# Encoder layer: norm weights spread by full-depth products, identity products ahead of them, first x tile in two halves

## The chip, the core and the metric

The kernel runs on one core of a Trainium2 chip. A core has five engines with a queue each, which run in order and wait for one another by semaphores: TensorE (PE; its weight loads are listed apart as PEld), VectorE (DVE), ScalarE (ACT), GpSimd (POOL) and SyncE (SP, which here issues all the DMAs). TensorE multiplies 128 rows deep, into PSUM, which has 8 banks of 128 x 512 float32. The metric is the time on the device in microseconds (us), the median of several runs.

## What is computed

The reference is one encoder layer, applied to two batches with shared weights: `x_prompt` (512 tokens) and `x_sample` (1024 tokens), 1024 channels, all float32. Cut to what matters here:

```python
def rmsnorm(x, g):
    y = x * lax.rsqrt(jnp.mean(x * x, axis=-1, keepdims=True) + EPS)
    return y * g

def encoder_layer(x, norm_g, w_in, ...):
    h = rmsnorm(x, norm_g)
    proj = h @ w_in                      # q, k, v, z of two attention branches, two gates
    ...                                  # neighbourhood attention (A), windowed attention (B)
    merged = sigmoid(ga) * oa + sigmoid(gb) * ob
    return x + merged @ w_out
```

The change touches how `h` of the prompt is begun: `norm_g` (1024 numbers, one for each channel) has to stand in every one of the 128 partitions, since a tile of x has 128 tokens in the partitions and the channels along the row.

## The kernel before, in words

The program has four phases: attention of the prompt, dense products of the prompt, then the same two for the sample. Float32 products are made of three products of `fp32r` parts: each operand is split into a high part (`whi`, `hh`; a copy on ACT) and a low part (`wlo`, `hl`; the operand less its high part, on DVE or POOL), and PE sums high by high, low by high and high by low (L764: three products for each of 8 depth steps, 24 for a tile of 128 tokens).

**The opening.** The prompt has four tiles `xt` of 128 tokens x 1024 channels (`norm_tile`, with t = 0 to 3). For a tile, in `rstd`: SP loads it (L460), ACT squares it with a running sum along the row (L463), POOL turns the sum into the mean plus epsilon (L467) and into the reciprocal root `nr` (L471). Then, in steps of 256 channels for t = 0 and of 512 for the others: DVE multiplies the tile by `nr` and by the norm weights (L523), PE transposes 128 x 128 pieces of it (L535, against the identity `ident`), ACT copies the transposed piece out of PSUM as `hh` (L540), and DVE makes `hl` (L545).

The norm weights get into all partitions in this way: SP loads them as one row of 1024 numbers into the first partition of the tile `rb` (L1799); PE multiplies a row of 128 ones (`one`, 1 x 128) by that row, in four products of 256 columns, one row deep (L1807), into two banks of PSUM; tile 0 reads the weights from PSUM (the `x` operand of its L523), and ACT copies each bank into `rb` (L1819), from where tiles 1 to 3 read them. A second copy of the weights, `gx`, holds the channels in the partitions (128 x 8, L1796). It is used in the sample's phase only, and its load has a late place in SP's queue.

The attention weights of the first group come in four pieces of 128 x 768 (L603; the first two into tiles `w`, the other two into tiles named `bias`), each split by ACT (`whi`, L605) and by DVE or POOL (`wlo`, L610). A tile's L764 needs pieces 1 to 4 in order, six products from each.

**What sets the order.** Nothing is issued as it is written. `Flow` collects all operations with a priority (the lower the sooner), their inputs and an estimated duration, then plays them through in its `run()`: at each planned moment an engine takes the ready operation with the lowest priority number, and where an operation has two engines to choose from (`wlo`, and other low parts and small sums), the one that is free sooner. So a new duration, or a new operation, moves others far behind it. The tables that matter here are `START` (priorities of the four loads of x), `NORM` (of the four tiles' work), `WAKE` and `WAKE_PRIO`. `wake()` puts `WAKE` groups of two PE instructions on the bank `d` ahead of other work; before, `WAKE` is 0, so that it puts none.

DMAs take 8 semaphores in turn, so SP holds the ninth DMA until the first has landed, and so on.

Of the kernel before, what the change touches and what calls it, by code (L numbers as in the profile page):

```python
# [29 lines left out]
SIDE = {5: 0, 8: 1, 11: 2, 15: 3}  # L30
CLASSIC_S = (0, 0, 0)
LEFT_PAD = 56
WAKE = 0
SOON = 10
RAW = {512: 2, 1024: 1}
WAKE_PRIO = 2
START = (-10, -6.5, -4, -3)
GATE = 2
FIRST_POOL = (0,)
# [1 line left out]
P = 128  # L41
# [313 lines left out]
def encoder_kernel(  # L355
# [4 lines left out]
    xt_p: bass.AP,  # L360
    xt_s: bass.AP,
    norm_g: bass.AP,
    norm_row: bass.AP,
    w_att: bass.AP,
    w_z: bass.AP,
    w_g: bass.AP,
# [49 lines left out]

    mhalf = cpool.tile([P, 8], F32, tag="mhalf", name="mhalf")
    dve.memset(mhalf, -0.5)
    one = cpool.tile([1, P], F32, tag="one", name="one")
    dve.memset(one, 1.0)  # L420
    gx = cpool.tile([P, KC], F32, tag="gx", name="gx")

    cpool.tile([P, LEFT_PAD], F32, tag="left_pad", name="left_pad")
# [18 lines left out]
    def wake():  # L442

        ps = bank("d")
        for i in range(WAKE):
            f.op(
                (("pe", 427),),
                lambda e, i=i: [pe.transpose(ps.t[:, j * P : (j + 1) * P], ident, ident) for j in range(2)],
                WAKE_PRIO, **({"into": [ps]} if i else {"new": [ps]}),
            )  # L450

    def rstd(pool, x, t, prio, load_prio, bufs, after=(), load_after=(), out=None):

        val = lambda shape, dt, tag, n: f.value(pool, shape, dt, tag, n)
        xt = val([P, D], F32, "xt", bufs)
        junk = val([P, D], mybir.dt.bfloat16, "junk", 1)
        ss, v = (val([P, 1], F32, "n" + n, bufs) for n in "sv")
        r = out or val([P, 1], F32, "nr", bufs)
        rv = lambda: r.t[:, t : t + 1] if out else r.t
        f.dma(lambda: nc.sync.dma_start(xt.t, x[t * P : (t + 1) * P, :]), 524288, load_prio, new=[xt], after=load_after)  # L460
        f.op(
            (("act", ACT_(D) + 93),),
            lambda e: act.activation(junk.t, xt.t, AF.Square, accum_out=ss.t), prio, new=[junk, ss], use=[xt], after=after,  # L463
        )
        f.op(
            (("pool", 164),),
            lambda e: nc.gpsimd.tensor_scalar(v.t, ss.t, 1.0 / D, EPS, op0=ALU.mult, op1=ALU.add),  # L467
            prio, new=[v], use=[ss],
        )
        f.op(  # L470
            (("pool", 464),), lambda e: nc.gpsimd.tensor_tensor(rv(), v.t, mhalf[:, :1], op=ALU.pow),  # L471
            prio, use=[v], **({"into": [r]} if out and t else {"new": [r]}),
        )
        return xt, r
# [1318 lines left out]


    f.stage(-1000, open=(r_h, d0["p"], rb_pool, early["p"], late["p"], norm_p), make=h_p)
    f.dma(lambda: nc.sync.dma_start(gx, norm_g), 4096, 1, into=[gx_v])  # L1796
    wake()
    gb = f.value(rb_pool, [P, NT_S], F32, "rb", 1)
    row = f.dma(lambda: nc.sync.dma_start(gb.t[:1], norm_row.unsqueeze(0)), 4096, START[0] + 0.1, new=[gb])  # L1799
    gains_row = []  # L1800
    for i in range(2):
        ps, made = bank("x"), []
        for j in range(2):
            cols, out = slice(i * 512 + j * 256, i * 512 + j * 256 + 256), slice(j * 256, j * 256 + 256)
            made.append(f.op(
                (("pe", 850),),
                lambda e, ps=ps, cols=cols, out=out: pe.matmul(ps.t[:, out], one, gb.t[:1, cols], start=True, stop=True),  # L1807
                NORM[0] - 1, hold=[gb], after=[row], **({"into": [ps]} if j else {"new": [ps]}),
            ))
        gains_row.append([ps, made])  # L1810
    for t in range(gp.nb):
# [64 lines left out]
def _layout(inp):  # L1876
# [15 lines left out]
    for m in range(8):  # L1892
# [11 lines left out]
        "xt_p": inp["x_prompt"][0][gp.perm].T.reshape(KC, P, NT_P),  # L1904
        "xt_s": inp["x_sample"][0][gs.perm].T.reshape(KC, P, NT_S),
        "norm_g": inp["norm_g"][0].reshape(KC, P).T,
        "norm_row": inp["norm_g"][0],
        "w_att": np.stack(groups),
        "w_z": np.stack(w_z),
        "w_g": np.stack(w_g),  # L1910
# [39 lines left out]
```

## Time and profile before

| | |
|---|---|
| runs, us | 1136.4, 1136.74, 1139.61 |
| median, us | 1136.74 |
| the profiled execution, us | 1139.25 |
| its span, first to last instruction, us | 1137.5 |
| mean granted TensorE clock | 0.998 of full |
| instructions | 18703 |
| bytes read and written in HBM | 137.66 MB and 51.92 MB |

A profile is one execution. Its pages list each engine's busy time; the view of waits says what ended an engine's idle time; the chain follows the work that ended last back from the last instruction; the timeline lists instructions by their start; the view by windows gives busy time of each engine in a stretch. Times are us from the first instruction. L numbers are lines of the kernel before; in the changed kernel the same lines stand from 1 line higher to 17 lines lower (L460 is L467, L463 is L474, L523 is L536, L535 is L548, L540 is L553, L545 is L558, L605 is L618, L610 is L623, L764 is L777, L1807 is L1825, L1819 is L1837).

### The profile page before, as it was taken

To read this page: it belongs to the slowest core of one execution; us is meant where nothing else is said; L and a number is where in the kernel's file an instruction comes from. 1 tells how busy PE (TensorE), PEld (TensorE's weight loads), DVE (VectorE), ACT (ScalarE), POOL (GpSimd) and SP (SyncE) were. 2 spreads that over 40 slices of the span, in tenths; PEclk is the share of its full clock that TensorE was granted. 3 is DMA by queue.
4 is the path that set the end of the run, shared out by engine and by line. 5 is a ranking of instruction groups with operands and counts; after the bars stand their busy time and mean duration, and the time that the engine had idled before them with its cause. 6 is when DMAs were issued, how large, how long until landed. Compare 5 with 4: busy or idle time off the path is not lost.

```text
span 1137.5 us, 18703 instructions
## 1 busy us (share of the span) xinstructions
PE 1121.8 (99%) x6079; PEld 975.1 (86%) x6079; DVE 856.8 (75%) x1988; ACT 651.4 (57%) x1499; POOL 339.3 (30%) x438
## 2 busy tenths in 40 slices
PE   8999999999999999999999999999999999999998
PEld 6999988888888889999999988988788888888877
DVE  5878797587776568787878889876988766767564
ACT  5777987644532247565769888877543435333430
POOL 3654433000011144434324343510333323123111
PEclk9999999999999999999999999999999999999999
DMA  7854543488785743121213214244888645756862
GB/s 257 273 159 138 185 115 103 107 254 257 246 286 202 249 138 91 29 61 29 82 41 93 73 38 119 50 131 138 288 261 237 206 158 191 278 197 224 262 208 93
DMA packets 139108, 186.11 MB, mean 164 GB/s; under 512 B 29897, under 2 KB 68561, under 8 KB 139010
## 3 DMA queue, kind: packets, MB, share of 16 engines
q1 hardware_dynamic: 139010, 184.91, 51.8%
q8 instruction: 48, 0.79, 0.3%
q14 instruction: 50, 0.41, 0.1%
HBM read 137.66 MB, written 51.92 MB: 167 GB/s over the span
## 4 chain that ended last, share of the span: by engine, by line
PE 90%; DMA 4%; DVE 2%; ACT 1%; issue 1%; SPq 1%; POOL 0%; ACTq 0%; DVEq 0%
PE p L764 26%; PE x L1293 8%; PE x L1295 8%; PE x L1294 8%; PE x L1066 5%; PE x L1029 5%; PE x L937 5%; PE p L1294 4%; PE p L1295 4%; PE p L1293 4%; PE d L1293 4%; PE d L1295 4%; PE d L1294 4%; PE x L864 2%; DMA w<-in_w_att_dram 1%; DMA U<-m_d 1%
## 5 line engine op out<-in xcount | busy, mean ns | idle before, releaser
L764 PE MATMUL p<-whi,hh 128*128 128x384 f32 x384 | 133.7, 348 | 0.0
L764 PE MATMUL p<-whi,hl 128*128 128x384 f32 x384 | 132.6, 345 | 0.0
L764 PE MATMUL p<-wlo,hh 128*128 128x384 f32 x384 | 132.0, 344 | 0.0
L1172 ACT ACTIVATE whi<-raw 128x512 fp32r<-128x512 f32 (+1 forms) x140 | 81.5, 600 | 73.0 <-PE x L1294 22.5
L981 ACT ACTIVATE sb<-sb,mx 128x384 f32<-128x384 f32 (+1 forms) x192 | 107.7, 565 | 16.9 <-DVE mx L972 16.6
L1294 PE MATMUL x<-T,whi 128*128 128x512 f32 x280 | 108.9, 389 | 0.0
L1293 PE MATMUL x<-T,whi 128*128 128x512 f32 x280 | 108.9, 389 | 0.0
L1295 PE MATMUL x<-T,wlo 128*128 128x512 f32 x280 | 108.9, 389 | 0.0
L764 PE MATMUL p<-whi,hb 128*128 128x384 f32 x384 | 107.6, 346 | 0.0
L1177 DVE TENSOR_TENSOR wlo<-raw,whi 128x512 fp32r<-128x512 f32 (+1 forms) x110 | 73.4, 678 | 34.5 <-ACT whi L1172 31.0
L1177 POOL TENSOR_TENSOR wlo<-raw,whi 128x512 fp32r<-128x512 f32 (+1 forms) x30 | 36.4, 1219 | 210.2 <-ACT whi L1172 210.2
L1040 DVE TENSOR_TENSOR pp<-x,pp 128x512 fp32r<-128x512 f32 (+1 forms) x136 | 82.6, 639 | 19.2 <-ACT pp L1035 18.5
L802 POOL TENSOR_TENSOR rs_r<-rs_v,mhalf 128x4 f32<-128x4 f32 (+1 forms) x72 | 80.7, 1121 | 5.7
L1293 PE MATMUL x<-hh,whi 128*128 128x512 f32 x200 | 78.4, 392 | 2.1 <-ACT fh L1440 2.1
L1035 ACT ACTIVATE pp<-x 128x512 fp32r<-128x512 f32 (+1 forms) x136 | 70.9, 561 | 15.2 <-PE x L1029 14.0
L1295 PE MATMUL x<-hh,wlo 128*128 128x512 f32 x200 | 78.5, 393 | 0.0
L1294 PE MATMUL x<-hl,whi 128*128 128x512 f32 x200 | 78.3, 392 | 0.0
L1066 PE MATMUL x<-pp,v 128*128 128x256 f32 (+1 forms) x368 | 75.8, 322 | 0.0
L764 PEld LDWEIGHTS p<-whi,hl 128*128 128x128 f32 x384 | 72.8, 190 | 1.3 <-issue 1.0
L764 PEld LDWEIGHTS p<-wlo,hh 128*128 128x128 f32 x384 | 73.0, 190 | 1.0 <-issue 0.7
L764 PEld LDWEIGHTS p<-whi,hh 128*128 128x128 f32 x384 | 73.0, 190 | 0.7 <-DVE v L812 0.3
L764 PEld LDWEIGHTS p<-whi,hb 128*128 128x128 f32 x384 | 69.1, 188 | 3.0 <-issue 1.3
(388 smaller groups left out, 2967.8 us busy)
## 6 DMA issues: line engine op xcount, KB each, us to landing
raw<-in_w_g_dram SPq DMA_DIRECT2D x84, 256.0 KB
w<-in_w_att_dram SPq DMA_DIRECT2D x46, 384.0 KB
raw<-in_w_z_dram SPq DMA_DIRECT2D x40, 256.0 KB
ot<-o_d SPq DMA_DIRECT2D x36, 256.0 KB
g_d<-C SPq DMA_DIRECT2D x34, 256.0 KB
fr<-in_w_g_dram SPq DMA_DIRECT2D x28, 256.0 KB
raw<-in_w_out_dram SPq DMA_DIRECT2D x28, 256.0 KB
out_dram<-C SPq DMA_DIRECT2D x19, 256.0 KB
```

The lines of the kernel that those rows point to most:

```text
L764: pe.matmul(ps.t[:, :GW], part[u](k), mv.t[:, c], start=k == 0 and m == 0, stop=k == KC - 1 and m == 2,)
L802: lambda e: nc.gpsimd.tensor_tensor(r.t[:, :nn], rv.t[:, :nn], mhalf[:, :nn], op=ALU.pow),
L937: pe.matmul(pss[2 * pair + i].t[:, :width], q.t[rows, u, at : at + P], kv[:, tiles[0] : tiles[-1] + 1 : step], start=n == 0, stop=n == 2,)
L981: act.activation(sb.t[:, :width], sb.t[:, :width], AF.Exp, bias=mx.t[:, i : i + 1], scale=-1.0, accum_out=sm.t[:, i : i + 1],)
L1035: lambda e, pt=pt, pp=pp, nn=nn: act.activation(pp.t[:, 0, :nn], pt.t[:, :nn], AF.Copy),
L1040: lambda e, pt=pt, pp=pp, nn=nn: dve.tensor_tensor(pp.t[:, 1, :nn], pt.t[:, :nn], pp.t[:, 0, :nn].bitcast(F32), op=ALU.subtract),
L1066: pe.matmul(out(), v.t[:, vs], mv(), start=first, stop=last)
L1172: (("act", ACT_(n)),), lambda e: act.activation(hi(), src(), AF.Copy), prio,
L1177: lambda e: engines[e].tensor_tensor(lo(), src(), hi().bitcast(F32), op=ALU.subtract), prio,
L1293: pe.matmul(out, hi.t[:, cs], mh(), start=first and k == 0, stop=False, **more)
L1294: pe.matmul(out, hi.t[:, cs], ml(), start=False, stop=False, **more)
L1295: pe.matmul(out, lo.t[:, cs], mh(), start=False, stop=last and k == len(ws) - 1, **more)
```

## The change

- `norm_row` is no longer an input. `gx` is loaded second instead, behind the first half of the first x tile.
- DVE multiplies the identity by each of the 8 columns of `gx`: eight diagonal tiles, side by side in `rb` (128 x 1024). The four products multiply a full 128 x 128 tile of ones by them: each result column is the sum of one diagonal column, which is the weight of that channel, in all partitions.
- `WAKE` is 6 and `WAKE_PRIO` -30: 12 products of the identity by itself, 128 x 128, float32, go first on PE. Before, the (unused) code had transposes there.
- The first tile of the prompt is loaded and squared in two halves of 512 columns, with two sums (`ns`, `nt`), which POOL adds in the instruction that adds epsilon. The factor 1/1024 moves from POOL into the scale of the Square (1/32) for all tiles, the sample's too.

```diff
-WAKE = 0
+WAKE = 6
...
-WAKE_PRIO = 2
+WAKE_PRIO = -30
...
-    one = cpool.tile([1, P], F32, tag="one", name="one")
-    dve.memset(one, 1.0)
+    ones = cpool.tile([P, P], F32, tag="ones", name="ones")
+    dve.memset(ones, 1.0)
...
-                lambda e, i=i: [pe.transpose(ps.t[:, j * P : (j + 1) * P], ident, ident) for j in range(2)],
+                lambda e, i=i: [
+                    pe.matmul(ps.t[:, j * P : j * P + P], ident, ident, start=True, stop=True) for j in range(2)
+                ],
...
+        halves = 1 if out or t else 2
+        loads, n = [], D // halves
+        for i in range(halves):
+            c = slice(i * n, i * n + n)
+            loads.append(f.dma(
+                lambda c=c: nc.sync.dma_start(xt.t[:, c], x[t * P : (t + 1) * P, c]), 512 * n, load_prio + 0.2 * i,
+                after=load_after, **({"hold": [xt]} if i else {"new": [xt]}),
+            ))
+        for i in range(halves):
+            c = slice(i * n, i * n + n)
+            f.op(
+                (("act", ACT_(n) + 93),),
+                lambda e, i=i, c=c: act.activation(junk.t[:, c], xt.t[:, c], AF.Square, scale=1.0 / 32, accum_out=sums[i].t),
...
-            lambda e: nc.gpsimd.tensor_scalar(v.t, ss.t, 1.0 / D, EPS, op0=ALU.mult, op1=ALU.add),
+            (lambda e: nc.gpsimd.tensor_scalar(v.t, ss.t, sums[1].t, EPS, op0=ALU.add, op1=ALU.add)) if halves == 2 else
+            (lambda e: nc.gpsimd.tensor_scalar(v.t, ss.t, 1.0, EPS, op0=ALU.mult, op1=ALU.add)),
...
-    f.dma(lambda: nc.sync.dma_start(gx, norm_g), 4096, 1, into=[gx_v])
+    f.dma(lambda: nc.sync.dma_start(gx, norm_g), 4096, START[0] + 0.1, into=[gx_v])
...
-    row = f.dma(lambda: nc.sync.dma_start(gb.t[:1], norm_row.unsqueeze(0)), 4096, START[0] + 0.1, new=[gb])
...
+            for k in (4 * i + 2 * j, 4 * i + 2 * j + 1):
+                diag = f.op(
+                    (("dve", 68 + 0.68 * P),),
+                    lambda e, k=k: dve.tensor_scalar(gb.t[:, k * P : k * P + P], ident, gx[:, k : k + 1], None, op0=ALU.mult),
...
-                lambda e, ps=ps, cols=cols, out=out: pe.matmul(ps.t[:, out], one, gb.t[:1, cols], start=True, stop=True),
+                lambda e, ps=ps, cols=cols, out=out: pe.matmul(ps.t[:, out], ones, gb.t[:, cols], start=True, stop=True),
```

The planner's estimate for a weight product goes from 850 to 450 ns. What the program now issues is shown at three places, all at the very start. On PE, before (a name is `out<-inputs`; `rb` the weights' row, `p` the projection):

```order
L1807 MATMUL x<-rb,one 128x256 x4
L535 MATMUL x<-ident,xt 128x128 x8
L764 MATMUL p<-whi,hh 128x384
L764 MATMUL p<-wlo,hh 128x384
L764 MATMUL p<-whi,hl 128x384
```

and in the changed program:

```order
L448 MATMUL d<-ident 128x128 x12
L1825 MATMUL x<-rb,ones 128x256 x4
L548 MATMUL x<-ident,xt 128x128 x6
L777 MATMUL p<-whi,hh 128x384
L777 MATMUL p<-wlo,hh 128x384
L548 MATMUL x<-ident,xt 128x128 x2
L777 MATMUL p<-whi,hl 128x384
```

The identity products stand first, and two products of the projection now stand ahead of the last two transposes of tile 0. Behind these rows, tile 1's eight transposes have moved from among tile 0's products to behind the last of them.

On ACT at the start, before (`junk,ns<-xt` is the Square; the one of 128x1024 in the sixth row is that of tile 1):

```order
L463 ACT_TABLE_LOAD
L463 ACTIVATE junk,ns<-xt 128x1024
L605 ACTIVATE whi<-w_124 128x768
L605 ACTIVATE whi<-w_126 128x768
L1819 ACTIVATE rb<-x 128x512
L463 ACTIVATE junk,ns<-xt 128x1024
L540 ACTIVATE hh<-x 128x2x128 x3
L605 ACTIVATE whi<-bias 128x768
L540 ACTIVATE hh<-x 128x2x128
L605 ACTIVATE whi<-bias 128x768
L1819 ACTIVATE rb<-x 128x512
```

and in the changed program:

```order
L474 ACT_TABLE_LOAD
L474 ACTIVATE junk,ns<-xt 128x512
L474 ACTIVATE junk,nt<-xt 128x512
L618 ACTIVATE whi<-w_133 128x768
L618 ACTIVATE whi<-w_137 128x768
L553 ACTIVATE hh<-x 128x2x128 x3
L1837 ACTIVATE rb<-x 128x512 x2
L618 ACTIVATE whi<-bias 128x768
L553 ACTIVATE hh<-x 128x2x128
L618 ACTIVATE whi<-bias 128x768
L474 ACTIVATE junk,ns<-xt 128x1024
```

The Square of tile 1 has moved from ahead of the first `hh` to behind the fourth `whi`, and both copies of the weights stand together behind the third `hh`.

On DVE at the start, before:

```order
L418 MEMSET mhalf 128x8
L420 MEMSET one 1x128
L523 SCALAR_TENSOR_TENSOR xt<-xt,nr,x 128x256 x2
L610 TENSOR_TENSOR wlo<-w_126,whi 128x768
L523 SCALAR_TENSOR_TENSOR xt<-xt,nr,x 128x256 x2
L545 TENSOR_TENSOR hl<-x,hh 128x2x128 x3
L523 SCALAR_TENSOR_TENSOR xt<-xt,nr,rb 128x512
L610 TENSOR_TENSOR wlo<-bias,whi 128x768
```

and in the changed program:

```order
L419 MEMSET ones 128x128
L1819 TENSOR_SCALAR rb<-ident,gx 128x128 x8
L536 SCALAR_TENSOR_TENSOR xt<-xt,nr,x 128x256 x4
L623 TENSOR_TENSOR wlo<-w_137,whi 128x768
L558 TENSOR_TENSOR hl<-x,hh 128x2x128 x3
L640 TENSOR_SCALAR gq<-gcol 128x2
L623 TENSOR_TENSOR wlo<-bias,whi 128x768
L558 TENSOR_TENSOR hl<-x,hh 128x2x128
L623 TENSOR_TENSOR wlo<-bias,whi 128x768
L536 SCALAR_TENSOR_TENSOR xt<-xt,nr,rb 128x512 x2
```

The second piece's `wlo` has moved behind all four multiplications of tile 0, and the two of tile 1 behind the `wlo` of the fourth piece.

On SP the loads of the weights' row and of the whole first tile are replaced by those of the first half, of `gx` and of the second half; then the order is the same for the next ten loads, without the later one of `gx`. Further back the order of DVE, ACT, POOL and SP differs through the prompt's attention and into its dense products, and some 19 operations move from DVE to POOL; from the later part of the prompt's dense products to the end it is the same on every engine.

More of the change, by code (lines that the diff above doesn't have):

```diff
@@ L362, in encoder_kernel @@
     norm_g: bass.AP,
-    norm_row: bass.AP,
     w_att: bass.AP,
@@ L456, in rstd @@
         junk = val([P, D], mybir.dt.bfloat16, "junk", 1)
-        ss, v = (val([P, 1], F32, "n" + n, bufs) for n in "sv")
+        ss, v, s2 = (val([P, 1], F32, "n" + n, 1 if n == "t" else bufs) for n in "svt")
+        sums = [ss, s2]
         r = out or val([P, 1], F32, "nr", bufs)
         rv = lambda: r.t[:, t : t + 1] if out else r.t
[L460 to L464, printed above, removed]
+        halves = 1 if out or t else 2
[11 more added lines that the diff above has]
+                lambda e, i=i, c=c: act.activation(junk.t[:, c], xt.t[:, c], AF.Square, scale=1.0 / 32, accum_out=sums[i].t),
+                prio, use=[xt], after=[*after, loads[i]], **({"new": [sums[1]], "into": [junk]} if i else {"new": [junk, ss]}),
+            )
         f.op(
             (("pool", 164),),
-            lambda e: nc.gpsimd.tensor_scalar(v.t, ss.t, 1.0 / D, EPS, op0=ALU.mult, op1=ALU.add),
-            prio, new=[v], use=[ss],
+            (lambda e: nc.gpsimd.tensor_scalar(v.t, ss.t, sums[1].t, EPS, op0=ALU.add, op1=ALU.add)) if halves == 2 else
+            (lambda e: nc.gpsimd.tensor_scalar(v.t, ss.t, 1.0, EPS, op0=ALU.mult, op1=ALU.add)),
+            prio, new=[v], use=sums[:halves],
         )
@@ L1795, in encoder_kernel @@
     f.stage(-1000, open=(r_h, d0["p"], rb_pool, early["p"], late["p"], norm_p), make=h_p)
-    f.dma(lambda: nc.sync.dma_start(gx, norm_g), 4096, 1, into=[gx_v])
+    f.dma(lambda: nc.sync.dma_start(gx, norm_g), 4096, START[0] + 0.1, into=[gx_v])
     wake()
     gb = f.value(rb_pool, [P, NT_S], F32, "rb", 1)
-    row = f.dma(lambda: nc.sync.dma_start(gb.t[:1], norm_row.unsqueeze(0)), 4096, START[0] + 0.1, new=[gb])
-    gains_row = []
+    gains_row, diag = [], None
     for i in range(2):
@@ L1803, in encoder_kernel @@
         for j in range(2):
+            for k in (4 * i + 2 * j, 4 * i + 2 * j + 1):
+                diag = f.op(
+                    (("dve", 68 + 0.68 * P),),
+                    lambda e, k=k: dve.tensor_scalar(gb.t[:, k * P : k * P + P], ident, gx[:, k : k + 1], None, op0=ALU.mult),
+                    NORM[0] - 1, use=[gx_v], **({"hold": [gb]} if k else {"new": [gb]}), after=[diag],
+                )
             cols, out = slice(i * 512 + j * 256, i * 512 + j * 256 + 256), slice(j * 256, j * 256 + 256)
             made.append(f.op(
-                (("pe", 850),),
-                lambda e, ps=ps, cols=cols, out=out: pe.matmul(ps.t[:, out], one, gb.t[:1, cols], start=True, stop=True),
-                NORM[0] - 1, hold=[gb], after=[row], **({"into": [ps]} if j else {"new": [ps]}),
+                (("pe", 450),),
+                lambda e, ps=ps, cols=cols, out=out: pe.matmul(ps.t[:, out], ones, gb.t[:, cols], start=True, stop=True),
+                NORM[0] - 1, hold=[gb], after=[diag], **({"into": [ps]} if j else {"new": [ps]}),
             ))
@@ L1906, in _layout @@
         "norm_g": inp["norm_g"][0].reshape(KC, P).T,
-        "norm_row": inp["norm_g"][0],
         "w_att": np.stack(groups),
```

## The prediction

> **What bounds the kernel now.** I read the page first, then the waits of the tensor engine (PE), then the chain that ended last, then the opening in order of time. The page's first part:
>
> ```profile
> PE 1121.8 (99%) x6079; PEld 975.1 (86%) x6079; DVE 856.8 (75%) x1988; ACT 651.4 (57%) x1499; POOL 339.3 (30%) x438
> ```
>
> PE is busy for 1121.8 of 1137.5 us, so a change can only win by removing PE idle time (15.7 us in all) or by making PE's own instructions shorter. The view of waits (who waited for what: us in total, times, longest) for PE:
>
> ```profile
> PE x L1807 <- DMA rb<-in_norm_row_dram: 4.6, 1, 4.6
> PE x L864 <- DVE qk L819: 2.4, 2, 1.9
> PE x L1293 <- ACT fh L1440: 2.1, 1, 2.1
> PE d L1294 <- DVE T L1177: 1.3, 1, 1.3
> PE x L535 <- DVE xt L523: 1.0, 1, 1.0
> PE p L1293 <- ACT whi L1172: 0.5, 1, 0.5
> ```
>
> The first and fifth row are the opening: 5.6 us. The others lie later; two rows of 0.2 follow. Then the chain over the opening (start, us, what):
>
> ```profile
> 1.94 6.16 DMA w<-in_w_att_dram
> ...
> 8.11 0.85 ACT whi L605
> ...
> 8.99 0.96 DVE wlo L610
> 9.95 0.40 DVE xt L523
> ...
> 10.39 1.15 PE x L535 x4
> 11.54 4.45 PE p L764 x15
> ```
>
> The second weight piece lands at 8.09; its low part (`wlo`, L610) stands on DVE ahead of the last two multiplications of x tile 0 (L523), and so holds PE's last four transposes until 10.39. From about 11.2 on PE has work without a break. But it is slow work at first. Rows of the timeline (start, duration):
>
> ```profile
> 14.86 0.52 PE L764 MATMUL p<-whi,hl 128*128 128x384 f32 x1
> ...
> 15.47 0.34 PE L764 MATMUL p<-wlo,hh 128*128 128x384 f32 x1
> ...
> 15.65 0.34 PE L764 MATMUL p<-whi,hl 128*128 128x384 f32 x1
> ...
> 18.65 0.35 PE L764 MATMUL p<-whi,hl 128*128 128x384 f32 x1
> ```
>
> Until 15.2 one product follows the other after 0.32 us (15 in 4.45 us, with the change near the end), from 15.47 on after 0.175 us. That is a clock at half rate, which the granted clock does not show here (it reads 1.00) but does show near the end of the kernel:
>
> ```profile
> 5.19:8.60 3.41, 3.41 (x10) 2.29 (x9) 0.87 (x2) 1.53 (x4) 2.53 (x3) 1.00 1.00 396
> 8.60:12.01 3.41, 2.40 (x11) 1.83 (x10) 2.84 (x7) 3.39 (x8) 0.75 (x2) 1.00 0.97 365
> 404.60:408.02 3.42, 2.12 (x10) 1.38 (x8) 2.81 (x5) 2.61 (x4) 3.25 (x3) 1.00 0.91 314
> 1083.79:1087.20 3.41, 1.32 (x6) 1.04 (x6) 1.93 (x4) 1.64 (x3) 0.00 (x0) 1.00 0.77 290
> 1087.00:1088.00 1.00, 1.00 (x4) 0.83 (x3) 0.77 (x2) 0.00 (x0) 0.00 (x0) 0.60 0.27 100
> 1090.00:1091.00 1.00, 1.00 (x5) 0.78 (x4) 0.87 (x2) 0.63 (x1) 0.00 (x0) 0.69 0.22 41
> ```
>
> (Stretch, length, then busy us of PE, PEld, DVE, ACT, POOL, then the granted clock.) 0.60 in 1087 to 1088 and 0.69 in 1090 to 1091 put the half rate from 1087.2 to 1090.6: one window of 3.4 us, after a window in which PE was busy for 1.32 of 3.41 us; and it ended after one full window. [...] In 5.19 to 8.60 PE was busy all the time with the products of one row (L1807), and still ran at half rate until 15.4. So such products did not raise the rate; the products of full depth (L764, from 11.2) did, 4.2 us later.
>
> [...]
>
> **The change, part by part.** These rows carry the durations (start, us, engine):
>
> ```profile
> 0.99 0.29 POOL masks.py:199 TENSOR_SCALAR_AFFINE_SELECT ident<-ident 128x128 f32<-128x128 f32 x1
> ...
> 4.29 1.06 ACT L463 ACTIVATE junk<-xt 128x1024 bf16<-128x1024 f32 x1 [2.30 <-DMA xt<-in_x_p_dram]
> ...
> 4.59 3.75 PE L1807 MATMUL x<-rb,one 1*128 1x256 f32 x8 [4.59 <-DMA rb<-in_norm_row_dram]
> ...
> 4.80 0.45 SPq L1796 DMA_DIRECT2D gx<-in_norm_g_dram  x1
> ...
> 5.25 0.19 ACT L463 ACTIVATION_READ_ACCUMULATOR junk<-xt 128x1 f32 x1
> ...
> 5.80 0.57 POOL L471 TENSOR_TENSOR nr<-nv,mhalf 128x1 f32<-128x1 f32 x1
> ...
> 6.86 0.87 DVE L523 SCALAR_TENSOR_TENSOR xt<-xt,nr,x 128x256 f32<-128x256 f32 x2 [5.86 <-PE x L1807]
> ...
> 8.86 0.58 ACT L1819 ACTIVATE rb<-x 128x512 f32<-128x512 f32 x1
> ...
> 10.51 0.99 ACT L540 ACTIVATE hh<-x 128x256 fp32r<-128x256 f32 x3
> ...
> 10.91 1.09 DVE L545 TENSOR_TENSOR hl<-x,hh 128x256 fp32r<-128x256 f32 x3 [0.18 <-ACT hh L540]
> ...
> 11.91 0.74 DVE L523 SCALAR_TENSOR_TENSOR xt<-xt,nr,rb 128x512 f32<-128x512 f32 x1
> ...
> 16.46 0.60 ACT L540 ACTIVATE hh<-x 128x512 fp32r<-128x512 f32 x1 [2.73 <-PE x L535]
> ...
> 17.09 0.69 DVE L545 TENSOR_TENSOR hl<-x,hh 128x512 fp32r<-128x512 f32 x1 [1.70 <-ACT hh L540]
> ```
>
> *The identity products.* They need only the identity, ready at 1.28, so PE starts near 1.45. Each float32 product is two passes: L1807's four are x8 in the trace. Eight passes of 256 columns take 3.75 us, about 0.446 each with the last one's drain left out; 128 columns are half, 0.223; 24 passes take 5.35 us and end at 6.8 at half rate. If they count as work, the rate rises 3.4 to 6.8 us after 1.45, at 5.0 to 8.3; I take the middle, 6.6, so they end at 6.7.
>
> *The weight products* now wait for them, not for a transfer: 6.7 against 4.59. At full rate eight passes of 0.223 end at 8.5. L523 began at 6.86, 0.49 us after the fourth pass of 0.446 from 4.59; now that is 6.7 + 0.89 + 0.45 = 8.05. The four multiplications of tile 0 then run in one piece, 0.475 each, to 9.95. Ahead of them lie eight multiplications of the identity on DVE. No row has that form; the nearest:
>
> ```profile
> L1013 DVE TENSOR_SCALAR sb<-sb,rs 128x256 f32<-128x256 f32 x33 | 11.0, 383 | 0.2
> ...
> L669 DVE TENSOR_SCALAR qk<-p,rs_r 128x128 f32<-128x128 f32 x5 | 1.7, 343 | 0.0
> ```
>
> Half of the first is 0.19 us, the second 0.34: eight take 1.5 to 2.7 us, and from the landing of `gx` (an estimate: near 4.0, behind the first half tile, since the whole tile had landed at 4.29) they end by 5.5 to 6.7. I take the lower, from SBUF like the new ones. The identity products hide either; without them the upper end would set the start of the last two weight products.
>
> *The x tile in two halves.* Half the data lands sooner (an estimate: 0.7 us, half of what 512 KB take), so the first Square runs under the second load. Two Squares of 0.60 (the 128x512 row) and two read-outs of 0.19 make 1.58 us against 1.25; the reciprocal root is ready near 6.1 against 6.37. With the weights at 8.05 this is worth nothing, and if the identity products were gone, at most 0.3 us. On SP one issue more, and `gx` (0.45) in the row's place (0.32), put the weight pieces back by some 0.5 us: the second lands at 8.6, its high part ends at 9.45, before DVE asks for it at 9.95.
>
> *What stands late now.* DVE: second `wlo` 9.95 to 10.9, then `hl` of tile 0, the first at 11.3; PE's third product needs it and starts at 11.6 (before: 11.98). From there 0.174 us each, with two short stalls for the `wlo` of the third and fourth piece: on ACT the third `hh` ends at 10.3, the two copies of the weights (L1819) at 11.5, third `whi` 12.35, fourth `hh` 12.7, fourth `whi` 13.55; on DVE the matching `wlo` end at 13.35 and 14.7. Tile 0's 24 products end at 15.8; before, with the eight transposes of tile 1 (0.9 us) already done, at 18.3. This is a lead of 1.6 us. But ACT now squares tile 1 only behind the fourth `whi`: 13.55 to 14.8 against 9.46. Then the root (0.93 us from the read-out, as 5.44 to 6.37), 15.75; two multiplications of 0.74, to 16.5 and 17.25; transposes, `hh` at 17.2 to 17.8; DVE has a sum and a copy (0.40 and 0.28) ahead of `hl`, 17.95 to 18.65. Tile 1's third product starts at 18.9; before, at 18.65. **The lead is gone**: PE idles 1.9 us of 15.8 to 18.9.
>
> Behind that the rows of PE are as dense as before, in another order; walked with the same durations, tile 2's products end 0.15 later. Before, the next thing was the shorter of the two waits for `qk` (2.4 less 1.9 is 0.5 us); now nine products of L1293 to L1295 stand ahead of those transposes and cover it. **Sum: +0.15 - 0.5, about -0.35 us.** The profiled execution took 1139.25 us (span 1137.5), so 1138.9. The runs shown lie at 1136.4, 1136.74 and 1139.61: two levels, and the profiled one is at the upper. I carry the difference to the median: 1136.4. The late landing at 8.09 may belong to the upper level alone; without it the old opening gains up to 0.9 (its second piece is then no longer on the path), the new one little, so the difference may be +0.5 at the median.
>
> **The rivals.**
>
> *The lead lasts.* If ACT's copies or the Square come sooner than I lay them out, the lead of 1.6 and the 0.5 stay: 1134.6; with the rate up at its earliest, 5.0, the identity products end 0.8 sooner: 1133.8. Against it: ACT's order is fixed and its rows sum as above.
>
> *The rate falls back.* Its place is the thin stretch from 15.8 to 18.9. The rows above bound the point where it decides: a window with 1.30 us idle of 3.42 (404.60) kept the rate, one with 2.09 idle lost it (1083.79). [...] The price: half rate until a window has filled again, 3.4 to 6.8 us, in the middle 16 products of 0.146 us more, 2.3 us: 1138.7, at most 3.1 us, 1139.5. This one is slower. [...]
>
> *It does not warm.* Float32 passes of an identity may count as little as the one-row products. Then the weight products end at 6.8 + 3.57 = 10.4, the last multiplication at 11.8, 1.85 later than above, and all behind it: 1138.2.
>
> *The new order costs.* Some 400 us of DVE, ACT, POOL and SP are in another order. In the waits above, the 0.5 of `qk` and the 0.5 of L1293 are all of any size that lies there; one more wait of the 1.9 or 2.1 us kind or two gives 1138.5 to 1140.5.
>
> **How the numbers follow.** Forecast 0.44, lead lasts 0.14, rate falls 0.16, no warming 0.12, order 0.14. 0.3% is 3.4 us, about what a measurement can tell from no change. Faster by more needs the whole lead and an early rate: 0.06. Slower by more: the upper ends of the fall and of the order, 0.09. Within: 0.85. The range reaches from the lead with an early rate, 1133.8, to the upper ends of the fall and the upper level of the runs, 1139.7.
>
> **What would show it.** Right: identity products from 1.4 to about 6.7; weight products over by 8.5; products 0.175 us apart from the first; Square of tile 1 at 13.5; PE idle near 16 to 18.9. Wrong: products 0.32 us apart after 12 (no warming) or after 18 (a fall); tile 1's third product before 18; new rows among PE's waits between 30 and 400 us.

## The result, and the profile after

| | before | after |
|---|---|---|
| median, us | 1136.74 (1136.4 to 1139.82) | 1148.6 (1145.06 to 1149.27) |
| after over before | | 1.0085, 95% interval 1.0065 to 1.0105 |
| the profiled execution, us | 1139.25 | 1149.27 |
| its span, us | 1137.5 | 1147.5 |

The change costs 0.85%, some 10 us (12 between the medians of these few runs); the forecast was 1136.4, with 1139.7 as its upper end. The first part of the page of the changed kernel:

```profile
PE 1126.4 (98%) x6103; PEld 976.6 (85%) x6103; DVE 860.0 (75%) x1977; ACT 653.0 (57%) x1503; POOL 348.1 (30%) x455
```

PE is busy 4.6 us longer (24 passes of the identity are 5.5), and its idle time has grown from 15.7 to 21.1 us. The opening is not where the time went. Its rows in the timeline of the changed kernel (start, us, engine):

```profile
1.34 5.49 PE L448 MATMUL d<-ident 128*128 128x128 f32 x24 [1.34 <-POOL ident masks.py:199]
...
6.63 2.01 PE L1825 MATMUL x<-rb,ones 128*128 128x256 f32 x8
...
8.00 1.66 DVE L536 SCALAR_TENSOR_TENSOR xt<-xt,nr,x 128x256 f32<-128x256 f32 x4 [2.60 <-ACT whi L618]
...
11.07 0.44 PE L777 MATMUL p<-whi,hl 128*128 128x384 f32 x1
...
12.76 1.07 ACT L474 ACTIVATE junk<-xt 128x1024 bf16<-128x1024 f32 x1
...
14.93 0.34 PE L777 MATMUL p<-whi,hl 128*128 128x384 f32 x1
...
15.69 1.38 PE L548 MATMUL x<-ident,xt 128*128 128x128 f32 x8 [0.42 <-DVE xt L536]
...
17.76 0.44 PE L777 MATMUL p<-whi,hl 128*128 128x384 f32 x1
```

The weight products take 2.01 us for eight passes, the full rate (before, 3.75 at half rate); the last product of tile 0 starts at 14.93; the third product of tile 1 at 17.76, which was 18.65 before. The loss is in later waits of PE. The view of waits (us in total, times, longest) of the changed kernel, first from 30 to 230 us, where before had one row of 0.5:

```profile
PE x L1849 <- POOL es L1010: 1.4, 1, 1.4
PE x L877 <- DVE qk L832: 1.1, 2, 0.7
PE x L1042 <- DVE sb L1026: 0.9, 1, 0.9
PE d L1306 <- ACT fc L1629: 0.7, 1, 0.7
```

then from 300 to 400 us, where before had one of 0.5 too:

```profile
PE x L1306 <- ACT hh L1185: 3.1, 1, 3.1
PE x L1307 <- DVE hl L1190: 0.5, 2, 0.3
```

The wait of 3.1 us ends at 363.8. The windows of the changed kernel around it (stretch, length, busy us of PE, PEld, DVE, ACT, POOL, granted clock, share and GB/s of the DMAs):

```profile
226.00:359.00 133.00, 133.00 (x588) 110.11 (x587) 95.72 (x188) 60.33 (x106) 7.41 (x5) 1.00 0.77 238
361.60:365.00 3.40, 0.96 (x3) 0.60 (x4) 2.16 (x4) 0.63 (x1) 0.00 (x0) 1.00 0.82 278
365.00:366.00 1.00, 1.00 (x5) 0.76 (x4) 0.69 (x2) 0.63 (x1) 0.00 (x0) 0.63 0.51 70
366.00:367.00 1.00, 1.00 (x4) 0.81 (x3) 0.67 (x2) 0.00 (x0) 0.00 (x0) 0.50 0.94 361
...
368.00:369.00 1.00, 1.00 (x5) 0.82 (x4) 0.43 (x1) 0.54 (x1) 0.00 (x0) 0.66 0.86 193
```

From 226 to 359 PE has no gap; then it idles, and behind that runs at half rate for 3.4 us (granted clock 0.50 from 365.3 to 368.7; such a stretch is called a half-rate window below), which costs another 1.7. Since PE's order is the same in both kernels from 226 us on, the same instruction can be looked up in both profiles. After is later than before by

| at (us, before) | 226 to 359 | 389 | 410 to 470 | 540 | 830 | 1099 on |
|---|---|---|---|---|---|---|
| later by, us | 3.7 | 8.7 | 9.1 | 10.2 | 12.1 | 10.0 |

So 3.7 us come in the prompt's attention, 5.0 at the wait of 364, the rest at waits for `qk` (531) and `T` (822 and 826); 2.1 come back at the end, where before has its own half-rate window (granted clock 0.50 from 1087.2 to 1090.6) and after hasn't.

Why PE waits at 364 is seen on SP. The timeline of SP in the kernel before (the last store `o_d` of the prompt's attention, the sample's bias copies `rpb_x`, then the first loads `ot` of the dense stage):

```profile
220.35 1.28 SPq L1102 DMA_DIRECT2D o_d<-ot__3275  x2
...
222.89 3.39 SPq L415 DMA_DIRECT2D rpb_x<-in_rpb_dram  x5
226.32 0.92 SPq L1535 DMA_DIRECT2D ot<-o_d  x2
```

and in the changed kernel:

```profile
222.95 8.23 SPq L414 DMA_DIRECT2D rpb_x<-in_rpb_dram  x12
...
233.16 1.27 SPq L1115 DMA_DIRECT2D o_d<-ot__3356  x2
...
236.42 0.91 SPq L1548 DMA_DIRECT2D ot<-o_d  x2
```

The last store of the prompt's attention comes 12.8 us later, and the first load of the dense stage, behind it in SP's queue, 10.1 us later, while PE is only 3.7 late. The last attention products on PE (L1066, in the changed kernel L1079) show why, before and after:

```profile
216.58 1.10 PE L1066 MATMUL x<-pp,v 128*128 128x512 f32 x4
...
227.78 1.10 PE L1079 MATMUL x<-pp,v 128*128 128x512 f32 x4
```

In the changed order 33 more rows of the trace (beside the 12 identity products) stand ahead of them in PE's queue, all of them products of the dense stage, 512 columns wide: they were pulled ahead, which kept PE busy and the attention waiting. One follows the other after 0.227 us, which makes 7.5 us; with the 3.7 that PE is late this is the 11.2 us by which the attention ends later. What the loads set in motion is a loop (load, DVE, store, load) that DVE's waits show in the kernel before, from 225 to 352 us:

```profile
DVE xt L488 <- DMA xt<-in_xt_s_dram: 11.2, 2, 5.8
DVE C L1166 <- DMA ot<-o_d: 6.8, 1, 6.8
...
DVE C L1166 <- DMA C<-g_d: 3.3, 1, 3.3
```

DVE waits some 23 us for transfers there while PE waits for nothing: PE had just enough dense products in stock to come to 356.3 us. The operand `hh` that it needs then is made on ACT, here before and after:

```profile
354.24 0.63 ACT L1172 ACTIVATE hh<-C 128x512 fp32r<-128x512 f32 x1 [4.57 <-DVE C L1166]
...
363.13 0.63 ACT L1185 ACTIVATE hh<-C 128x512 fp32r<-128x512 f32 x1 [4.56 <-DVE C L1179]
```

Before, that fitted by about a microsecond.

### The profile page after: what moved, and what is told of

Same layout as the page of the kernel before. It is cut to its first block, busy times and chain, and to the rows that moved or that the text cites. A ratio compares the mean times of both kernels' runs of the same rounds, so it can differ in the third digit from the quotient of the medians.

```text
span 1147.5 us, 18777 instructions
## 1 busy us (share of the span) xinstructions
PE 1126.4 (98%) x6103; PEld 976.6 (85%) x6103; DVE 860.0 (75%) x1977; ACT 653.0 (57%) x1503; POOL 348.1 (30%) x455
## 4 chain that ended last, share of the span: by engine, by line
PE 80%; DMA 7%; DVE 5%; issue 3%; ACT 2%; POOL 2%; SPq 0%; DVEq 0%; POOLq 0%; ACTq 0%
PE p L777 23%; PE x L1307 7%; PE x L1308 7%; PE x L1306 7%; PE x L1079 5%; PE x L1042 5%; PE x L950 4%; PE d L1306 3%; PE d L1308 3%; PE d L1307 3%; PE p L1307 3%; PE p L1306 3%; PE p L1308 3%; PE x L877 2%; DMA U<-m_d 1%
## 5 line engine op out<-in xcount | busy, mean ns | idle before, releaser
L1190 DVE TENSOR_TENSOR wlo<-raw,whi 128x512 fp32r<-128x512 f32 (+1 forms) x110 | 75.8, 699 | 31.6 <-ACT whi L1185 25.9
L1079 PE MATMUL x<-pp,v 128*128 128x256 f32 (+1 forms) x368 | 75.7, 321 | 0.0
L1042 PE MATMUL x<-ident,sb 128*128 128x128 f32 x496 | 69.7, 273 | 0.9 <-DVE sb L1026 0.9
```

Source lines behind the costliest of these rows:

```text
L1042: pe.transpose(pt.t[:, u * P : (u + 1) * P], sbs[i].t[:, c * P : (c + 1) * P], ident)
L1079: pe.matmul(out(), v.t[:, vs], mv(), start=first, stop=last)
L1190: lambda e: engines[e].tensor_tensor(lo(), src(), hi().bitcast(F32), op=ALU.subtract), prio,
```

## The experiments

Ratios are to runs of the kernel before on the same chip, with 95% intervals. The time given for a kernel is its median. L numbers in a run's views are lines of that run's kernel.

**1. The order alone, the opening alone.** In the first kernel the planner is told another duration, after which every engine has before's order behind the opening:

```diff
-                (("pe", 450),),
+                (("pe", 900),),
```

> All instructions of the change, with the work behind the opening in the order of the kernel before: the planner is told 900 ns for a weight product instead of 450, and from tile 0's first product on each engine's order is that of before. Theory 1, the order behind the opening costs the time: the opening itself gains 1 to 2 us, so 1134 to 1136.5 us (ratio 0.998 to 1.000), no wait of 3.1 us near 364 us, the last L1066 near 217 us. Theory 2, the new opening instructions cost it later by themselves (clock, transfers, contention): 1144 to 1150 us.

1143.49 us, ratio 1.0043 (1.0027 to 1.0059): as neither theory has it. The opening lost 1.9 us in this order, since the second piece's `wlo` stands ahead of tile 0's last two multiplications and PE idled 2.56 us in 8.43 to 11.84. Its windows:

```profile
8.43:11.84 3.41, 0.85 (x5) 0.42 (x5) 2.54 (x4) 3.23 (x7) 2.27 (x3) 0.89 0.97 377
12.60:13.60 1.00, 1.00 (x5) 1.00 (x4) 0.86 (x3) 1.00 (x3) 0.00 (x0) 0.50 1.01 411
```

The rate fell back, the rival of the prediction, though not in the changed kernel's order. It also waited at 360, 380 and 392 us (1.3 to 1.4 each) and 2.2 us at 416, with a half-rate window behind it, so this run doesn't tell the two theories apart. In the second kernel before's instructions stand in the order of the change: the planner sees the change's operations, which issue nothing or what before issues.

```diff
-                    lambda e, k=k: dve.tensor_scalar(gb.t[:, k * P : k * P + P], ident, gx[:, k : k + 1], None, op0=ALU.mult),
+                    lambda e: None,
...
-                lambda e, ps=ps, cols=cols, out=out: pe.matmul(ps.t[:, out], ones, gb.t[:, cols], start=True, stop=True),
+                lambda e, ps=ps, cols=cols, out=out: pe.matmul(ps.t[:, out], one, gb.t[:1, cols], start=True, stop=True),
```

> The opening instructions of before (no identity products, products of one row, a whole x tile) with everything in the order that the change gives. Theory 1: 1146 to 1151 us (ratio 1.008 to 1.012), with the wait of some 3 us near 365 us and the last L1066 near 229 us. Theory 2: 1136 to 1139 us.

1147.55 us, 1.0089 (1.0069 to 1.0110): the order alone costs what the change costs. From 340 to 400 us its PE waits

```profile
PE x L1304 <- ACT hh L1183: 4.8, 2, 3.1
```

and it is 5.0 us late at 226, against 3.7 of the changed kernel: the new opening itself is worth 1.3 us there.

**2. Other orders of the same opening.** One number decides between a handful of orders. The whole first tile, and the planner's old duration:

```diff
-        halves = 1 if out or t else 2
+        halves = 1
```

> One part of the change undone: x tile 0 in one load and one Square again. This also lets the planner come to a third order, in which the last prompt product of L1066 stands 60 rows earlier on PE than in the changed kernel and 27 (beside the identity products, 39) earlier than before. Theory 1, what counts is how many dense products stand ahead of the last attention products: the prompt's attention ends at or before 217 us, no wait near 364 us, 1133 to 1138 us. Rival, each new order has its own waits of a few us at places that this count does not tell: anything from 1136 to 1150 us. Theory 2 (the new instructions cost it): 1144 to 1150 us.

```diff
-                (("pe", 450),),
+                (("pe", 850),),
```

> All instructions of the change; the planner is told 850 ns for a weight product (the number of the kernel before) instead of 450, which gives a fourth order: the last prompt product of L1066 stands 48 rows earlier on PE than in the changed kernel. Theory 1 with the count of rows: attention over by 219 us, 1133 to 1138 us. Rival (each order has its own waits): 1136 to 1150 us. Theory 2: 1144 to 1150 us.

1140.55 us, 1.0033 (1.0017 to 1.0048), and 1147.27 us, 1.0081 (1.0061 to 1.0100). The count of rows is no measure of the time: the first misses by 2.6 us, the second by 9, though its last attention product starts at 215.0 (before 217.3) and its loads at 223.3; the operand of 354.2 was started at 358.3. From the first load to that operand its loop takes 135.0 us, in the kernel before 127.9: an early end of the attention doesn't mean an early end of the loop. In its profile (one of its fastest executions, 1144.63 us) some 3.5 us are lost at the same join as in the changed kernel, to a wait of 1.4 us and a half-rate window from 360.7 on.

**3. Is it the loop?** More work for PE, less and more for SP's queue.

```diff
+                    if first and k == 0 and len(stored) == 16 and len(extra) < 8:
+                        extra.append(k)
+                        for j in range(2):
+                            pe.matmul(ps.t[:, :P], ident, ident, start=True, stop=True)
```

> The changed kernel with 16 more float32 products of the identity (32 passes of 0.11 us, 3.6 us of PE work that nobody uses), two ahead of each of the first eight groups of dense products behind the last store of the prompt's attention, from about 235 to 262 us. Theory A, from 230 to 420 us a loop of loads and DVE work sets the time and PE only waits for it at 364 us: the extra work is taken out of that wait, which shrinks from 3.1 us to nothing, and the time stays within 1.0 us of the changed kernel, 1147 to 1149.5 us (the half-rate window behind the wait may go too, then down to 1146). Theory B, PE's own work and order set the time: 3.6 us more, 1151 to 1153 us.

```diff
+                        nc.sync.dma_start(dst, ot.t[e * 64 : e * 64 + 64])
+                        for h, lo in [soon.pop(0) for _ in range(2)] if nt == NT_P and soon else ():
+                            expand(gs, h, lo)
```

(In e6 the copies are left out at their old place.)

> The changed kernel with the sixteen copies of the sample's bias (L414) issued two by two behind the first eight of the prompt's attention stores, from 159 us on, instead of behind the attention, at 215 to 240 us, where they take 0.66 us each on SP's queue ahead of the first loads of the dense stage. No engine's order changes but SP's. Theory A (a loop of loads sets 230 to 420 us): the loop starts up to 8 us earlier, the wait of 3.1 us at 364 and the half-rate window behind it go, 1141 to 1145 us. Theory B (the waits come from the order of the engines' work): 1147 to 1150 us.

```diff
-                f.dma(lambda h=h, lo=lo: expand(geo, h, lo), 196608, prios[h], after=after[h // 2]) for lo in range(2)
+                    lambda h=h, lo=lo: [expand(g, h, lo) for g in ((geo, gp) if geo is gs and h < 4 else (geo,))],
```

> The kernel before with eight more such copies (of the prompt's bias, again; nobody reads them) among the sixteen at 213 to 231 us: some 5 us more of SP's queue ahead of the dense stage's loads, nothing else changed. Theory A: PE, which before waited for nothing until 384 us, comes to wait near 364 us, and the time grows by 3 to 6 us, 1140 to 1144 us. Theory B: PE's work and order are as before, so 1137 to 1138.5 us.

The times of the first two are those of theory A, and the third got the wait that theory A has, at a higher price. With 3.6 us more for PE: 1148.38 us (after: 1148.6); the wait at 364 shrank to 1.0 us and the clock stayed at 1.00 in its windows behind it:

```profile
361.60:365.00 3.40, 2.41 (x11) 1.69 (x9) 2.19 (x4) 0.63 (x1) 0.44 (x1) 1.00 0.93 266
365.00:369.00 4.00, 3.77 (x16) 2.91 (x16) 1.86 (x3) 0.67 (x2) 0.00 (x0) 1.00 0.89 242
```

PE was 0.6 us ahead of the changed kernel there, and lost some 3.6 us at a new wait, for `whi` at 395.3, and the half-rate window behind it (396.2 to 399.6):

```profile
PE p L1313 <- ACT whi L1188: 1.8, 1, 1.8
```

Later waits shrank in turn. That the sum is so near the changed kernel's is partly chance.

With the copies early: 1143.23 us, 1.0042 (1.0026 to 1.0058), and no wait of PE from 300 to 400 us. With eight more copies in the kernel before, and nothing else changed (the copies also move 0.8 MB, which was not told apart from their place in the queue): 1145.75 us, 1.0062 (1.0047 to 1.0076), more than the 3 to 6 us expected, and its waits of PE have the row that the changed kernel has:

```profile
PE x L1297 <- ACT hh L1176: 3.1, 1, 3.1
```

**4. A better opening in the old order.** Before's order by hand, with the whole first tile, identity and full-depth products, and the second `wlo` behind the four multiplications, all else in before's order:

```diff
+                    *[go() for go in (late_lo if t == 0 and k0 == 6 else [])],
...
+            if e == "dve" and not late_lo:
+                late_lo.append(go)
```

> The opening of the change in the order of the kernel before, without what made the first such run lose 1.9 us by 18 us: x tile 0 is loaded whole again, and DVE does the four multiplications of tile 0 ahead of the second piece's low part. If the products then run at full rate from the first on, tile 0's products end near 14 us and all behind is 1 to 2 us earlier than before. Theory A: the loop of loads starts that much earlier too, 1135 to 1136.5 us. Theory C, the lead is lost again before 230 us to DVE, ACT and the loads: 1137 to 1139 us.

1144.03 us, 1.0041 (1.0023 to 1.0060), outside both. Everything on PE was 1.47 us earlier than before until 352 us; then, in its waits and windows:

```profile
PE x L870 <- DVE qk L825: 3.2, 3, 2.2
PE x L1299 <- ACT hh L1178: 3.1, 1, 3.1
```

```profile
358.00:359.00 1.00, 0.61 (x1) 0.19 (x1) 0.63 (x1) 0.33 (x1) 0.00 (x0) 0.80 0.91 234
359.00:360.00 1.00, 0.90 (x3) 0.79 (x3) 0.06 (x1) 0.11 (x1) 0.00 (x0) 0.50 0.33 127
...
413.00:414.00 1.00, 0.94 (x4) 0.95 (x5) 0.20 (x2) 0.33 (x2) 0.91 (x1) 0.61 0.97 379
```

Behind each of the two waits (3.1 and 2.2 us) the granted clock reads 0.50 for some 3.4 us, from 358.6 and from 413.2 on. The first wait is longer than before's, which was none, for two reasons: PE came 1.5 us earlier, and `hh` was started 3.5 us later than in the first profile of before. That the wait has 3.1 us in several kernels has a plain reason: the last two `hh` start 5.2 us apart (357.94 and 363.13 in the changed kernel, 352.52 and 357.70 in e8), and PE has 2.1 us of products between them. A PE that is further ahead waits at the one before as well, as in e2 (1.7 us). Four kernels asked what sets the end of the loop: e8 with the early copies (the edit of e6), before again, e8 with 18 identity products, and e8 with `norm_row` kept as an unread input.

```diff
-WAKE = 6
+WAKE = 9
```

```diff
+    norm_row: bass.AP,
...
+        "norm_row": inp["norm_g"][0],
```

> The kernel of e8_old_order_fast with the sample's copies issued early, as in e6_early_expand. In e8_old_order_fast all of PE ran 1.47 us earlier than before until 352 us and then waited 3.12 us at 358 us. Theory A (the loop of loads from 230 us on sets the end of that stage): the wait and the half-rate window behind it go, and the lead of 1.5 us is kept: 1136 to 1139 us. Theory D (the loop gets longer for another reason when the opening changes, and its start doesn't matter): 1142 to 1145 us.

> The kernel before, unchanged, for a second profile of it. Ratio 0.998 to 1.002. If the loop of loads varies from run to run, the end of its stage (the store of L1520 that came at 314.8 us) moves by 1 to 4 us and PE has a wait near 364 us; if it is the same each time, 314.8 us within 0.5.

> The kernel of e8_old_order_fast with 18 products of the identity instead of 12: 12 passes of 0.11 us more, so the lead of 1.47 us shrinks to about 0. Theory D1, the loop of loads depends on the lead (PE frees the buffers in other places of the stream): as the kernel before, 1137 to 1140 us. Theory D2, the new opening slows the loop by itself (its tensors and buffers lie elsewhere): 1144 to 1147 us.

> The kernel of e8_old_order_fast with the input norm_row kept, though nothing reads it, so that the inputs lie in device memory as before. If their place sets how fast the loads run, 1135 to 1138 us; if not, 1142 to 1145 us as e8_old_order_fast.

| kernel | median, us | ratio (interval) | first load of `ot` | `hh` started | PE's wait for it |
|---|---|---|---|---|---|
| before, first profile | 1136.74 | | 226.3 | 354.2 | 0 |
| e10, before again | 1139.18 | 1.0006 (0.9990 to 1.0022) | 226.2 | 355.8 | 0.1 |
| after | 1148.6 | 1.0085 (1.0065 to 1.0105) | 236.4 | 363.1 | 3.1 |
| e2, order alone | 1147.55 | 1.0089 (1.0069 to 1.0110) | 238.7 | 366.9 | 3.1 |
| e6, after with early copies | 1143.23 | 1.0042 (1.0026 to 1.0058) | 233.3 | 358.8 | 0 |
| e7, before with more copies | 1145.75 | 1.0062 (1.0047 to 1.0076) | 232.1 | 362.2 | 3.1 |
| e8 | 1144.03 | 1.0041 (1.0023 to 1.0060) | 225.8 | 357.7 | 3.1 |
| e12, e8 with `norm_row` | 1142.66 | 1.0030 (1.0015 to 1.0045) | 223.6 | 354.1 | 1.1 |
| e11, e8 with `WAKE = 9` | 1141.56 | 1.0032 (1.0016 to 1.0048) | 224.8 | 356.2 | 1.9 |
| e9, e8 with early copies | 1138.29 | 1.0004 (0.9988 to 1.0021) | 218.1 | 351.4 | 0 |

A start of the loads 6 to 12 us later made `hh` 5 to 13 us later than in the first profile of before (the least in e6, where the copies were out of the way), and a start 8 us earlier (e9) made it 3 earlier, with no wait of PE. Within one program the loop's end moves from run to run: 1.6 us between the two profiles of before, 3.6 between e8 and e12, whose loads started 2.3 apart. Nor does the start alone set the end: from the first load to `hh` it is 125.6 us in e6, 126.7 in the changed kernel, 127.9 and 129.6 in the two of before, 133.3 in e9. The place of `norm_row` changes nothing that is measured. `WAKE = 9` did not shrink the lead (1.49 us at 209), so that run says nothing on its two theories.

**5. Work that nobody needs, in front of the waits.**

```diff
+                    for j in range({256: 10, 824: 5}.get(len(calls), 0)):
+                        pe.matmul(ps.t[:, :P], ident, ident, start=True, stop=True)
...
+                if nt == NT_S:
+                    for j in range({0: 5}.get(len(sample_qk), 0)):
+                        pe.matmul(pt.t[:, :P], ident, ident, start=True, stop=True)
```

> The kernel of e8_old_order_fast with 20 products of the identity that nobody uses: ten (20 passes, 2.2 us) ahead of the group of dense products in front of the wait of 3.1 us at 358 us, five (1.1 us) ahead of the sample's first transposes of qk at 413 us, where PE waited 2.2 us, five ahead of the group in front of the wait at 1092 us. Theory E, waits of over some 2 us cost a window at half rate on top: the work itself hides in the waits and the two half-rate windows (358.4 to 362 and 413.5 to 416.7) go, so it is faster with more work: 1140 to 1142.5 us against 1142.7 to 1144.0. Theory D (the loop of loads ends later, the rate doesn't matter): 1143 to 1146 us.

> The kernel before with ten such products: five ahead of the sample's first transposes of qk (a wait of 1.9 us in one profile, of 1.1 and 0.6 us in the other), five ahead of the group in front of the wait of 2.1 us at 1086 us. Theory E: the half-rate window at 1087 us, which one of the two profiles has, never comes: 0 to 1.5 us faster, ratio 0.9985 to 1.000. Theory D: ratio 1.000 to 1.002.

> The kernel of e9_fast_early with fifteen such products: five ahead of the first and of the second of the sample's transposes of qk (waits of 1.9 and 2.2 us), five ahead of the group in front of the wait at 1086 us. Theory E: its slower runs lose their half-rate windows, 1136 to 1138 us, ratio 0.9975 to 0.9995. Theory D: 1138 to 1140 us.

The three have this edit on e8, on before (the two fives) and on e9 (a third five, at the second `qk`). With 4.4 us of such work the kernel of e8 takes 1138.03 us, 1.0003 (0.9991 to 1.0014), below what either theory expected. That is 4.6 to 6.0 us less than without (e12, e8) by the medians, 3.1 to 4.3 by the ratios to before on the same chip; two half-rate windows, at 1.7 each as in the changed kernel, are worth 3.4. Its windows have the full clock at both places:

```profile
354.00:358.00 4.00, 4.00 (x19) 3.33 (x18) 1.99 (x4) 1.12 (x2) 0.00 (x0) 1.00 0.65 226
358.00:362.00 4.00, 4.00 (x20) 3.30 (x19) 1.94 (x3) 0.77 (x2) 0.00 (x0) 1.00 0.71 271
410.00:413.00 3.00, 2.39 (x15) 2.07 (x14) 2.33 (x9) 0.71 (x3) 0.13 (x1) 1.00 0.22 62
413.00:417.00 4.00, 4.00 (x25) 4.00 (x24) 2.46 (x9) 0.55 (x2) 1.98 (x3) 1.00 0.16 45
```

But in that execution the loop also ended 2.3 us earlier than in e8's (`hh` at 355.4), within what it varies by, and the lead was down to some 0.3 us, since the opening fell back to half rate (granted clock 0.50):

```profile
11.12:14.53 3.41, 3.23 (x10) 3.23 (x11) 3.25 (x7) 2.90 (x7) 0.70 (x2) 0.50 1.02 413
```

Without the added 2.1 us PE would have come to that `hh` at 356.1, just as it was ready. So at 358 us this profile doesn't show that the work kept the rate. At 413 it left a wait of 0.6 us, which without its 1.1 us would have been 1.7. How the gain splits between the rate, the loop and the lead is open. In the kernel before the same trick gives 1138.11 us, 1.0000 (0.9986 to 1.0014), and in e9 1137.91 us, 0.9991 (0.9978 to 1.0003): the best of all, and not told apart from no change.

Last, the early copies and the two fives together, on the changed kernel and on that of e3:

> The changed kernel with both remedies: the sample's copies issued early (e6_early_expand, 1143.2 us) and ten products of the identity in front of two waits (at 413 and 1093 us, as in e14_before_filled). If the loop's late start and the half-rate windows are what can be mended without touching the order, 1141.0 to 1143.0 us, and the 3.5 to 4 us that are left against the kernel before are the waits inside the prompt's attention (at 42, 148, 149 and 225 us, 3.9 us) and at 817 to 821 us, which are of the order itself. If the order costs nothing beside the loop and the rate: 1138 to 1139.5 us.

> The kernel of e3_whole_tile (x tile 0 whole, a third order, 1140.6 us) with the same two remedies. Its attention has fewer waits (1.4 us between 30 and 230), so if the two remedies are what it lacks: 1136.5 to 1138.5 us, ratio 0.998 to 1.000; if its order costs by itself: 1139 to 1141 us.

1142.42 us, 1.0046 (1.0032 to 1.0061): both remedies leave the changed kernel 5 us behind; the early copies gave all of the gain. The mean granted clock of its profiled execution is 1.0, so that what is left is not the rate. The waits of the order are still in its list:

```profile
PE d L1322 <- DVE T L1202: 1.6, 1, 1.6
PE x L1864 <- POOL es L1019: 1.4, 1, 1.4
PE p L1321 <- ACT whi L1197: 1.4, 1, 1.4
...
PE x L1051 <- DVE sb L1035: 0.9, 1, 0.9
```

The third order with both: 1138.31 us, 1.0004 (0.9990 to 1.0017). Nothing here beats the kernel before by more than can be told.

## Why the prediction was wrong

- *Identity and weight products*: to 6.7 and 8.5 predicted; 6.83 and 8.64 in the profile. Right. That the rate would be up behind the identity products was right too: eight weight passes in 2.01 us, against 3.75 before. The 3.4 to 6.8 us that the prediction gives the rise were its author's estimate, and no run shows such a rule; here the first product starts at 1.34, and the products run at full rate from some 6.8 us on.
- *The multiplications of tile 0*, 8.05 to 9.95: 8.00 to 9.66. *The third product* at 11.6 and full rate from there: 11.07. Tile 0's products end at 15.8: the last starts at 14.93.
- *The Square of tile 1* at 13.55, its third product at 18.9, "The lead is gone": 12.76 and 17.76. The opening is up to 1.1 us better than forecast, since PE and ACT ran a little ahead at each step. The rate did not fall at 15.8 to 18.9: from the end of tile 0's products (15.27) to 18.9 PE idled 0.63 us, not 1.9.
- **"Behind that the rows of PE are as dense as before, in another order" is the step that failed.** It looked at PE's rows up to about 30 us, and took a dense PE for an unharmed one. Apart from 3.6 us of new waits PE is as dense as before until 359 us, because dense products of the next stage were moved ahead of the attention's, and it then stands without operands, since the loop that makes them had started 10 us later. The order alone, with before's instructions, costs 1.0089 (e2).
- The sum of the prediction has +0.15 for what lies behind the opening and -0.5 for a wait covered. In their place stand, in the two profiles: 3.7 us by 226 (3.6 of it new waits), 5.0 at 364 (3.1 and 0.5 of waiting, the rest mostly the half rate), 3.4 up to 830, and -2.1 at the end.
- *The rival "the new order costs"* (1138.5 to 1140.5) was the right one and mis-sized. It priced one or two waits of the kinds that the kernel before has, 1.9 and 2.1 us. It had no row on what the order does to SP's queue and to the stage that the queue feeds, and no price for the clock behind a new wait, though it stood in the rival beside it.
- *The rival "the rate falls back"* had the kind of loss right and the wrong place. It goes by two rows of the kernel before (1.30 us idle of 3.42, rate kept; 2.09 of 3.41, rate lost). In the changed kernel the rate fell at 365.3 us, behind 3.41 us with 2.18 us of idle time, and in e1's order in the opening (granted clock 0.50 in 12.60 to 13.60). Its 3.4 to 6.8 us at half rate were an estimate too; at 365.3 they were 3.4.
- What could have been read beforehand: that DVE waits 23 us for transfers between 225 and 352 us while PE waits for nothing, so that PE lives on its stock there; and that 33 more rows of PE stand ahead of the attention's last product. From the same rows it follows that a lead of PE ends at 356 us, unless the loop starts earlier too.

What stays open: why the loop's end varies by up to 3.6 us between executions, what beside its start sets its length (125.6 to 135.0 us), and so why the order of e4, with an early attention, is as slow as the changed one. The waits inside the prompt's attention, 3.6 us, were shown to belong to the order (e2 and e16 have them too) and not followed further.

## What to carry to other kernels

A busy engine in front of a join (a place where it needs what another chain makes) is no sign of health: look for what the join waits for, when that chain starts, and by how much the busy engine's stock of work outlasts it. Where a scheduler lays out the program, compare the places of the chains' starts in the queues (stores and loads on the DMA queue above all) before and after, and not the density of the bound engine. A lead won ahead of such a join is lost at the join, and may cost more than it won: in e8 the granted clock was 0.50 for some 3.4 us behind the longer wait, and e8 and e12 are 0.3 to 0.4% slower than the kernel before.

## What the runs showed of the hardware

- The rate of PE fell behind stretches in which PE had idled. In the kernel before the granted clock is 0.50 from 1087.2 to 1090.6 us, behind 3.41 us with 2.09 us idle; it stayed at 1.00 behind 3.42 us with 1.30 us idle (404.60 to 408.02). In the changed kernel it is 0.50 from 365.3 to 368.7, behind 3.41 us with 2.18 us idle (361.86 to 365.27). The length of a wait alone doesn't tell: the wait of 2.3 us before 417.7 in the changed kernel was followed by no fall, the 1.8 us before 395.3 in e5 by half rate from 396.2 to 399.6. What decides it is not shown. Two lines around the wait before 417.7, then the one ahead of the half rate in e5:

```profile
413.05:416.47 3.42, 2.36 (x11) 1.62 (x9) 3.36 (x6) 3.42 (x7) 2.32 (x3) 1.00 0.91 292
416.47:419.88 3.41, 2.15 (x14) 1.92 (x14) 2.98 (x11) 0.68 (x3) 2.50 (x4) 1.00 0.29 100
...
392.77:396.19 3.42, 1.61 (x7) 0.72 (x6) 0.93 (x2) 0.95 (x2) 0.00 (x0) 1.00 1.02 358
```

- Behind 12 float32 products of a full 128 x 128 identity PE ran at full rate in the changed kernel: their 24 passes of 128 columns took 5.49 us, the eight weight passes of 256 columns right behind them 2.01 us. Behind the products one row deep in the kernel before it did not: these ran from 4.59 to 8.3 us, eight passes of 256 columns in 3.75 us, and the rate stayed half until 15.4 (products 0.32 us apart ahead of that, 0.175 behind it). The stretch that the prediction read, 5.19 to 8.60, had transposes in its last 0.3 us.
- In four of the five sets of runs of the kernel before, those with a mean granted clock of 1.0 are faster by 1.7 to 2.7 us in the mean than those below it (in the largest 1137.2 against 1139.4 us, 19 and 16 runs); in the fifth they are 0.4 slower. So part of what looks like noise in this kernel may be how many of its waits have a half-rate window behind them; that is not shown.
